# First mixer by feature halves: a column order of the modulation, written out by hand

## The chip, the cores and the metric

The kernel runs on one core of a Trainium2 chip. The metric is the device time of one execution in microseconds, median of the runs. The engines named below are TensorE (PE; its weight loads are PEld), VectorE (DVE), ScalarE (ACT), GpSimd (POOL) and SyncE (SP), which here issues nearly all loads.

## The reference, cut to what matters

Two transformer blocks run one after the other on 256 tokens of 1024 features. The first block takes a condition vector `c` and makes six rows of 1024 values from it (`mod = silu(c) @ w_ada + b_ada`, a matrix of 1024 x 6144). The change is about the first two, `shift_m` and `scale_m`:

```python
mod = (jax.nn.silu(c) @ w_ada[l] + b_ada[l])[:, None, :]
shift_m, scale_m, gate_m, shift_f, scale_f, gate_f = jnp.split(mod, N_MOD, axis=-1)
h = rms_norm(x, g_mix[l]) * (1.0 + scale_m) + shift_m
x = x + gate_m * hybrid_mixer(h, w_in[l], ...)
h = rms_norm(x, g_ffn[l]) * (1.0 + scale_f) + shift_f
x = x + gate_f * hierarchical_moe(h, ...)
```

The mixer multiplies `h` by `w_in` (1024 x 2896) and cuts the product into queries, keys and values of two attentions and into an indexer (`iq`, 512 columns; `ik` and its weights, 72 columns), which picks 64 keys for each token. The mixture of experts chooses 2 of 32 experts for each token; each expert has three matrices of 1 MB. The second block (a recurrent mixer and a dense feed-forward) is not touched by the change.

## The kernel before, in words

**Order.** The kernel is a straight-line program for the five engines. A planner, which has a cost for each instruction, puts the instructions into the queue of their engine. Instructions that are marked (`keep_in_program_order`; the helpers `held`, L76, and `held_pe`, L95, mark while the list `holding` is filled, with two entries also those of PE) stay in the order of the program text. All loads on SP are marked, so they are issued in the text's order, and each waits there until its buffer is free.

**Head of the first mixer.** `ada_piece` (L125) loads 1 MB of `w_ada`: 2 rows of each partition, 1024 columns of one of the six outputs, 4 KB a row. The head loads four pieces of output 0 (shift), then `xt` (the tokens, 1 MB, L158), four pieces of output 1 (scale), then the columns of `w_in` in 1 MB pieces with 2 KB rows. `ada(v)` (L328) multiplies each piece as it lands, four products of 32 rows side by side; after the fourth piece it copies the sums (L351) and turns them into columns with 16 products against `selh` (each 64 weight columns), and adds the bias (L357). Feature `f` lies on partition `f // 8`, so that a column of `w_in` needs all of `w_ada`'s columns of both outputs before any feature can be used. Meanwhile `xt` is normed (L395, L388, L437) and turned (L400). `scaled` (L414) makes the eight feature tiles: `hTh` on ACT (L423), `full` on DVE (L425), and the rest `hTl` on POOL or DVE (L426).

**Projections.** Every large product is made of three: high by high, high by low, low by high (`mm3`, L110). `hilo` (L85) cuts the weights: ACT copies the high part (L86), DVE subtracts (L87). One step of `proj_fm` (L467) is a cut of two feature tiles of 512 columns and 24 products of 256 columns; four steps make a projection. `proj_ik` (L498) does the 72 indexer columns and the 8 forget columns with 24 products. `main` runs one cut ahead of the products. The order of the work is a string of letters (L885): `iiqikqqFqXFXbb...`, i = indexer queries, q = queries of the second attention, k = `proj_ik`, F = a step of `forget` (its first turns the indexer's key and weights, L622 to L628, and then works on the forget gate), X = a step of the indexer for tokens 128 to 255 (the first makes the scores `p_dot`, L680, and ReLU, L681; then DVE sums them, L685, and picks the best 64 in 8 rounds, L691 and L692).

**Experts.** `load_experts` (L228) takes the 96 matrices in the order of 8 units of 4 experts, gates, then ups, then downs. The kind of buffer of load `i` is `RING[i % 21]`: 1 is a buffer of `raw`, 2 of `raw2`, 3 of `raw3`. 16 loads go out at the letter W, five more (L911) behind the first block's mixer, when `raw3` exists. `raw3` has five buffers, and the first of them holds `xn2`, the normed tokens, until they are cut into three parts (L1015 to L1019). The fifth of those loads, which is load 20, takes that buffer. Unit 0 then calls `load_experts` after its gates, its ups and its downs, four loads each (L1335 to L1351).

**Router.** Around L1041 everything is marked. The text has, for the second half of the tokens: squares, `turned`, `normed`, `warm(5)`, `logits(1)`, `experts(0)`, `rank(0)`, `warm(3)`, `places(0)`, `gather_t(0)`. `warm(n)` (L102) issues n constant products of 128 x 128.

## Time and profile before

| What | Value |
|---|---|
| median of 3 runs | 719.64 us (718.5 to 719.88) |
| the profiled execution's own time | 719.28 us |
| its span | 717.6 us |
| mean granted TensorE clock | 0.966 |
| PE busy | 651.5 us (91%) |
| DVE, ACT, POOL busy | 397.3, 301.2, 46.1 us |
| moved by DMA | 196.94 MB |

A row of the timeline gives start and duration in us, then engine, line and operation, what is written from what is read, its shape and how many; in square brackets stands the idle time of the engine ahead of it and what ended it. Fp32 products are recorded twice each, so 16 records are 8 products. Ends of PE instructions are modelled, starts are not. "x" behind a group counts records.

### The profile page before, as it was taken

What the parts mean: (1) busy time and instruction counts of PE and PEld (TensorE: products, weight loads), DVE (VectorE), ACT (ScalarE), POOL (GpSimd) and SP (SyncE); (2) the same over time, 40 slices, a digit from 0 to 9 for tenths busy, and PEclk for the clock granted to TensorE, in tenths of its full rate; (3) what the DMA queues carried; (4) which work ended last, traced back from release to release, by engine and by line L of the source; (5) the groups of instructions that cost most, each with busy time, mean ns of one, the idle gap of its engine ahead of it and who ended that gap; (6) DMA issues with size and microseconds to landing.
All of it is one profiled execution on the core that took longest, in us unless ns stands there. A gap on an engine that the chain in (4) does not pass through costs nothing. (4 is left out here: it accounts for less than half of the span.)

```text
span 717.6 us, 13286 instructions
## 1 busy us (share of the span) xinstructions
PE 651.5 (91%) x5485; PEld 508.2 (71%) x5485; DVE 397.3 (55%) x753; ACT 301.2 (42%) x505; POOL 46.1 (6%) x71
## 2 busy tenths in 40 slices
PE   4799999999988789569889999999999999999996
PEld 0498787767845454324545699987899999898994
DVE  2277967877651242123123489788575555555555
ACT  1456454654631020101101587756474444444445
POOL 7010000001000000000000423100000000000001
PEclk9899999999998999879999999999999999999998
DMA  9999669998579999999999997535346555550001
GB/s 340 374 375 393 229 261 333 306 419 295 226 317 416 418 419 418 414 418 398 418 418 393 377 365 295 177 117 167 128 141 206 194 196 200 168 187 1 1 1 58
DMA packets 69203, 196.94 MB, mean 274 GB/s; under 512 B 7550, under 2 KB 33219, under 8 KB 57350
## 3 DMA queue, kind: packets, MB, share of 16 engines
q1 hardware_dynamic: 67558, 195.30, 72.5%
q8 instruction: 53, 0.87, 0.5%
q10 hardware_dynamic: 1216, 0.30, 0.2%
q0 software_dynamic: 352, 0.28, 0.1%
q14 instruction: 24, 0.20, 0.1%
HBM read 194.81 MB, written 1.05 MB: 273 GB/s over the span
## 5 line engine op out<-in xcount | busy, mean ns | idle before, releaser
L100 PE MATMUL p_gu<-Xl,wguh 128*128 128x256 f32 x352 | 99.8, 284 | 0.0
L100 PE MATMUL p_gu<-Xh,wgul 128*128 128x256 f32 x352 | 99.3, 283 | 0.0
L100 PE MATMUL p_gu<-Xh,wguh 128*128 128x256 f32 x352 | 98.9, 283 | 0.1
L100 PEld LDWEIGHTS p_gu<-Xl,wguh 128*128 128x128 f32 x352 | 67.5, 192 | 0.5
L100 PEld LDWEIGHTS p_gu<-Xh,wguh 128*128 128x128 f32 x352 | 67.1, 192 | 0.7 <-ACT Xh L1392 0.4
L100 PEld LDWEIGHTS p_gu<-Xh,wgul 128*128 128x128 f32 x352 | 67.4, 192 | 0.3 <-DVE wgul L87 0.2
L100 PE MATMUL p_gu<-eg,xg 128*32 128x256 f32 x576 | 44.3, 467 | 22.1 <-PEq L1311 19.9
L100 PEld LDWEIGHTS p_gu<-eg,xg 128*32 128x32 f32 x576 | 24.0, 132 | 43.2 <-issue 36.1
L1163 ACT ACTIVATE sl<-p_gu 128x256 f32<-128x256 f32 x9 | 3.5, 384 | 121.5 <-PE p_gu L100 121.5
L1164 DVE TENSOR_TENSOR sl<-sl,p_gu 128x256 f32<-128x256 f32 x9 | 3.8, 421 | 79.5 <-ACT sl L1163 79.5
L87 DVE TENSOR_TENSOR wdnl<-wdn,wdnh 128x1024 fp32r<-128x1024 f32 x22 | 27.0, 1225 | 32.4 <-ACT wdnh L86 32.4
L100 PE MATMUL p_w<-hTh,wih 128*128 128x256 f32 x128 | 37.5, 296 | 2.5 <-ACT wih L86 2.5
L87 DVE TENSOR_TENSOR wgul<-wup,wguh 128x1024 fp32r<-128x1024 f32 x22 | 27.0, 1225 | 21.3 <-ACT wguh L86 20.2
L86 ACT ACTIVATE wdnh<-wdn 128x1024 fp32r<-128x1024 f32 x22 | 23.3, 1058 | 36.5 <-PE p_gu L100 35.9
L100 PE MATMUL p_dn<-ed,aT 128*32 128x512 f32 (+2 forms) x304 | 33.0, 573 | 5.9 <-ACT aT L1171 5.9
L87 DVE TENSOR_TENSOR wgul<-wgt,wguh 128x1024 fp32r<-128x1024 f32 x22 | 27.0, 1225 | 19.8 <-ACT wguh L86 19.8
L86 ACT ACTIVATE wguh<-wgt 128x1024 fp32r<-128x1024 f32 x22 | 23.3, 1061 | 33.7 <-PE p_gu L100 18.2
L100 PE MATMUL p_w<-Xh,w2h 128*128 128x256 f32 x128 | 37.0, 289 | 0.5 <-ACT w2h L86 0.3
L100 PE MATMUL p_w<-Xh,w2l 128*128 128x256 f32 x128 | 36.2, 284 | 0.6 <-DVE w2l L87 0.6
L100 PE MATMUL p_w<-hTl,wih 128*128 128x256 f32 x128 | 36.5, 287 | 0.0
L100 PE MATMUL p_w<-Xl,w2h 128*128 128x256 f32 x128 | 36.4, 284 | 0.1
L100 PE MATMUL p_w<-hTh,wil 128*128 128x256 f32 x128 | 36.2, 288 | 0.0
(624 smaller groups left out, 1546.4 us busy)
## 6 DMA issues: line engine op xcount, KB each, us to landing
eg<-in_w_gate_dram SPq DMA_DIRECT2D x32, 1024.0 KB
eu<-in_w_up_dram SPq DMA_DIRECT2D x32, 1024.0 KB
ed<-in_w_down_dram SPq DMA_DIRECT2D x28, 1024.0 KB
wada<-in_w_ada_dram SPq DMA_DIRECT2D x24, 1024.0 KB
w<-in_w_in_dram SPq DMA_DIRECT2D x11, 1024.0 KB
wgt<-in_w_gate_up_dram SPq DMA_DIRECT2D x11, 1024.0 KB
wup<-in_w_gate_up_dram SPq DMA_DIRECT2D x11, 1024.0 KB
wdn<-in_w_down_dram SPq DMA_DIRECT2D x11, 1024.0 KB
```

The costliest lines, as they stand in the source:

```text
L86: held(act.activation(hi, src, AF.Copy))
L87: held(eng.tensor_tensor(lo, src, f32(hi), op=OP.subtract))
L100: held_pe(pe.matmul(o, lhsT, rhs, start=start, stop=stop, skip_group_check=True))
L1163: act.activation(st.s[:st.n], st.b[:st.n, 0:256], AF.Silu)
L1164: dve.tensor_tensor(st.s[:st.n], st.s[:st.n], st.b[:st.n, 256:512], op=OP.mult)
```

## The change

It does these things:

- The feature order of the first mixer changes: feature `f` of half `h` lies on partition `(f - 512 h) // 4`, four to a partition in each half (`load_cols`, the biases, `turn_half`). Shift and scale come in halves of 512 columns (`ada_half`, two loads of 1 MB each, 2 KB rows; class `Cols` with its three steps `prod`, `cols`, `turn`; the turn has four products against `sel4`).
- The loads go in this order: scale half 0, `xt`, shift half 0, first half of `iq`'s rows, first half of `bq`'s rows, `wik`, `w_bf` (two loads), scale half 1, shift half 1, then the other halves of `iq` and `bq`.
- The head is written out in a fixed order on PE, ACT, DVE and POOL, up to the indexer's scores and ReLU; the indexer stands ahead of the rest of `bq`. The string starts with `qFFX` behind that.
- `RING` has 20 entries for the first pass, `AGAIN` has 21 for the later ones: load 20 takes a `raw` buffer (that of load 0), load 24 takes `xn2`'s. Unit 0 issues 4, then 5 loads.
- The router has `warm(1)` and `warm(2)` for `warm(5)` and `warm(3)`.

```diff
-RING = [1, 1, 2, 2, 1, 1, 1, 1, 1, 2, 1, 1, 2, 2, 1, 1, 3, 3, 3, 3, 3]
+RING = [1, 1, 2, 2, 1, 1, 1, 1, 1, 2, 1, 1, 2, 2, 1, 1, 3, 3, 3, 3]
+AGAIN = RING[:4] + [3] + RING[4:]
...
-    for _ in range(4):
-        ada_piece(0)
+    ada_half(1, 0)
     tc.keep_in_program_order(nc.sync.dma_start(xt, dram("x", 0, [[D, 128], [128 * D, 2], [1, D]])))
-    for _ in range(4):
-        ada_piece(1)
+    ada_half(0, 0)
+    w_iq = [load_cols("win768_0", 768, 512, 0)]
+    w_bq = [load_cols("win1352_0", 1352, 512, 0)]
+    w_ik = load_cols("wik", 1280, 72)
...
+    ada_half(1, 1)
+    ada_half(0, 1)
...
+    class Cols:
+        def __init__(self, v, h):
+            self.v, self.h, self.p = v, h, bank([128, 512], "p_ada")
+        def prod(self, q):
+            for r in range(4):
+                mm(self.p[32 * r:32 * r + 32], csr[:, 4 * q + r, :], wada[self.v, self.h][q][:, r], q == 0, q == 1)
+        def cols(self):
+            self.part = a1.tile([128, 512], FT, name="part", tag="fin", bufs=3)
+            held(act.activation(self.part.rearrange("p (j n) -> p j n", j=4),
+                                self.p.rearrange("p (n j) -> p j n", j=4), AF.Copy))
+        def turn(self):
...
+            for j in range(4):
+                mm(p[:, j:j + 1], self.part[:, 128 * j:128 * j + 128], sel4, j == 0, True)
+            held(dve.tensor_tensor(modcol[:, v, hs], p, bcol[:, v, hs], op=OP.add))
...
+    first[1].prod(0)
+    turn_half(0)
+    first[1].prod(1)
+    first[1].cols()
+    first[1].turn()
+    turn_half(1)
...
+    run = ahead_of(st)
+    tokens(range(2))
+    run()
+    tokens(range(2, 4))
+    for gen in (st, sq_):
+        ahead_of(gen)()
+    ik_ = cut_ik()
+    second = [Cols(1, 1), Cols(0, 1)]
+    second[0].prod(0)
+    second[0].prod(1)
+    second[0].cols()
+    run = ahead_of(sq_)
+    run(jjs=(0,))
+    second[0].turn()
+    second[1].prod(0)
+    second[1].prod(1)
+    second[1].cols()
+    run(jjs=(1,))
+    run = ahead_of(st)
+    second[1].turn()
+    prod_ik(*ik_, range(4))
+    tokens(range(4, 6))
+    run()
+    tokens(range(6, 8))
+    run, run2 = ahead_of(st), ahead_of(sq_)
+    run()
+    prod_ik(*ik_, range(4, 8))
+    run2()
+    next(gates)
+    next(index1)
...
-    for c in "iiqikqqFqXFXbbYYbb...":
+    for c in "qFFXbbYYbb...":
...
-    warm(5)
+    warm(1)
+    experts(0)
     logits(1)
-    experts(0)
     rank(0)
-    warm(3)
+    warm(2)
...
         gate_up(st, "u")
-        load_experts(n)
+        load_experts(n + (k == 0))
```

## Rows read from the trace of the kernel before

**Rows 1.** The page, its part with 40 equal slices of the span: PE and GB/s.

```profile
PE   4799999999988789569889999999999999999996
...
GB/s 340 374 375 393 229 261 333 306 419 295 226 317 416 418 419 418 414 418 398 418 418 393 377 365 295 177 117 167 128 141 206 194 196 200 168 187 1 1 1 58
```

**Rows 2.** Waits of SP's queue: us in total, times, longest.

```profile
SPq L252 <- DVE xn L1019: 20.4, 1, 20.4
```

**Rows 3.** Timeline of SP, loads of experts around the router.

```profile
177.78 1.97 SPq L252 DMA_DIRECT2D eu<-in_w_up_dram  x4
200.30 2.50 SPq L252 DMA_DIRECT2D ed<-in_w_down_dram  x4
```

**Rows 4.** Timeline of PE: first gates of the experts, downs of the last unit.

```profile
192.12 3.66 PE L100 MATMUL p_gu<-eg,xg 128*32 128x256 f32 x64
...
397.59 3.21 PE L100 MATMUL p_dn<-ed,aT 128*32 128x512 f32 x32 [0.53 <-ACT aT L1171]
```

**Rows 5.** Timeline of all engines, head of the first mixer.

```profile
17.18 1.06 ACT L395 ACTIVATE prob<-xt 128x1024 f32<-128x1024 f32 x1
...
22.06 0.75 DVE L437 TENSOR_SCALAR prob<-xt,rsr 128x1024 f32<-128x1024 f32 x1
...
28.25 1.06 PE L100 MATMUL p_ada<-wada,csr 128*32 128x512 f32 x8 [1.11 <-DMA wada<-in_w_ada_dram]
29.38 0.60 ACT L351 ACTIVATE part<-p_ada 128x512 f32<-128x512 f32 x1 [8.22 <-PE p_ada L100]
...
30.03 1.21 PE L100 MATMUL p_col<-selh,part 128*64 128x1 f32 x32 [0.72 <-ACT part L351]
...
33.68 1.23 DVE L87 TENSOR_TENSOR wil<-win,wih 128x1024 fp32r<-128x1024 f32 x1 [0.86 <-ACT wih L86]
...
33.70 0.58 PE L100 MATMUL p_w<-hTh,wih 128*128 128x256 f32 x1 [2.46 <-ACT wih L86]
...
34.90 1.07 ACT L86 ACTIVATE wih<-win 128x1024 fp32r<-128x1024 f32 x1
```

**Rows 6.** Windows of 5 us: busy us of PE, PEld, DVE, ACT, POOL, clock, DMA, GB/s.

```profile
10.00:15.00 5.00, 3.60 (x20) 0.40 (x16) 0.00 (x0) 0.00 (x0) 4.92 (x12) 1.00 1.03 410
...
40.00:45.00 5.00, 5.00 (x44) 5.00 (x44) 4.66 (x8) 2.99 (x4) 0.79 (x1) 1.00 1.04 376
...
70.00:75.00 5.00, 5.00 (x44) 5.00 (x43) 4.90 (x17) 2.04 (x3) 0.00 (x0) 1.00 0.62 216
```

**Rows 7.** Timeline of PE and ACT, from the indexer's keys to the next projection.

```profile
50.04 0.28 PE L100 MATMUL p_ik<-hTh,ikh 128*80 128x256 f32 x1
...
55.68 0.60 PE L100 MATMUL p_dup<-aqk,dup 80*128 80x256 f32 x2
...
59.70 2.00 PE L100 MATMUL p_dot<-aqk,iqT 64*128 64x256 f32 x16
...
62.25 2.04 ACT L681 ACTIVATE prob<-p_dot 128x512 f32<-128x512 f32 x4
...
62.69 0.38 PE L642 MATMUL p_lft<-ident,lf 128*8 128x128 f32 x2 [0.99 <-DVE lf L638]
...
62.83 0.36 PE L100 MATMUL p_w<-hTh,wih 128*128 128x256 f32 x1
```

**Rows 8.** Windows of 1 us, columns as in the windows of 5 us.

```profile
36.00:37.00 1.00, 1.00 (x6) 1.00 (x6) 1.00 (x2) 1.00 (x2) 0.74 (x1) 0.50 0.96 239
...
181.00:182.00 1.00, 1.00 (x7) 1.00 (x6) 0.86 (x6) 0.36 (x2) 0.00 (x0) 0.52 1.07 451
...
185.00:186.00 1.00, 1.00 (x11) 1.00 (x11) 0.00 (x0) 1.00 (x1) 0.00 (x0) 1.00 1.06 451
```

**Rows 9.** Timeline of PE and ACT in the router.

```profile
182.05 2.34 PE L108 MATMUL p_warm<-ones,ident 128*128 128x128 f32 x10
182.29 0.60 ACT L959 ACTIVATE h<-p_tr 128x512 f32<-128x512 f32 x1 [0.90 <-PE p_tr L561]
...
184.18 2.01 PE L100 MATMUL p_lg<-wr,h 128*128 128x36 f32 x16
```

## The prediction

> **What bounds the kernel now.** I read the page's slices first, then the waits of SP, then the timelines. In the slices [rows 1] the PE digit is 9 nearly throughout the second half of the span, where the loads are far from full: that part is PE's, and the change does not touch it. Slices 13 to 22 (the experts, about 200 to 390 us) are the ones with full loads, 414 to 419 GB/s, and a PE below 9. So the first question is which of the two sets the end of the experts.

> The loads have a hole: SP stands 20.4 us before one load for `xn2` [rows 2]. It is load 20, issued at 200.30, while the four before it went out at 177.78 [rows 3]. From 200.30 on, 76 MB are to come: 76 x 1.0486 MB at 418 GB/s [rows 1] are 190.7 us, which ends at 391, and some 2 us later the last piece has landed. PE wants the last downs at 397.59 and waits there for ACT's `aT`, not for a load [rows 4]. So the loads have about 4 us to spare, and the end of the experts is set by PE's own chain, which starts with unit 0's gates at 192.12 [rows 4]. What brings that start forward is gained; what brings only loads forward is not.

> The start at 192.12 hangs on the first mixer, where PE is busy in nearly every window from 40 us on, with DVE close by at 70 us (4.90 of 5) [rows 6]. Before that PE starves: its first projection product is at 33.70, 5.45 us behind the landing of the last of eight `w_ada` pieces at 28.25 [rows 5].

> **The head of the mixer.** *Loads.* Rows of 4 KB come at 410 GB/s (2.56 us a MB), the mix with 2 KB rows at 376 (2.79) [rows 6]. [...] I take 2.79. The fifth MB then lands near 17.8, against 28.25 for the ninth. `iq` and `bq` follow at 20.5 and 23.3. For `wik` and `w_bf`, small rows, I allow 2.5. The second halves of scale and shift land by 31.5 and 37.0, `iq`'s at 39.8, `bq`'s at 42.5.

> *Start.* `xt` is third and lands near 12.3. From the first square to the end of the second norm it was 17.18 to 22.81, 5.6 us [rows 5], so `xn` stands at 18.0. The text puts `turn_half(0)` ahead of the last shift product, so this product runs about 19 to 20.5, the copy takes 0.60, the turn less than the 1.21 of 32 small records [rows 5], since it has 8; the shift stands at 22.3. From there to steady products it was 2.4 us; I take 2.5. First products: 24.8, which is 8.9 ahead of 33.70.

> *From there to the indexer's scores.* Before, the scores `p_dot` came at 59.70 [rows 7]. Now PE has ahead of them: seven groups of 24 products; `proj_ik`, 24 more; four groups of `w_ada` products at 1.06 [rows 5]; two turns, 1.0 as an estimate from the 1.21; the duplication and turn of the keys, 0.7. From 50.04 to 55.68 [rows 7] there are 48 products, 0.1175 each, so a group takes 2.82, and the sum is 8 x 2.82 + 4.2 + 1.0 + 0.7 = 28.5. Before, six groups, `proj_ik` and the 0.7 were enough.

> *Waits that the fixed order adds.* ACT stands in text order. The copy `cols` of the second scale half comes ahead of the cut of `bq`'s next step, so that cut waits for the `w_ada` products, and PE for the cut: 0.60 + 1.07 + 1.23 [rows 5], about 2.9. Behind the ACT cut stand the next cuts and the tiles `hTh`. Before the second shift the cut's DVE half stands ahead of the bias addition: about 0.7. The duplicated keys need a copy, 0.4. Together 4.0: the scores at 57.3 with a full clock.

> *The clock.* [...] From 33.70 to 50.04 there are 120 products, 14.1 at 0.1175 each, so the fall cost 2.2. [...] Bounds: no fall, and two of 2.2; I take half a fall, 1.1. The scores: 58.4, 1.3 earlier.

> *Behind the scores.* Before, PE waited 0.99 for `lf` and took the next projection at 62.83, 3.1 behind the scores [rows 7]. Now the same group can follow right behind the 2.0 of the scores if its cut is done, at 60.4: 2.4 earlier. If the planner leaves the cut behind the four ReLUs (2.04) it is 0.5 + 2.04 + 1.07 + 1.23 = 4.8 behind: 0.4 later than before. I take the first, as nothing orders the cut behind the ReLUs. DVE's sums get their first ReLU about 3 us earlier than after 62.25 [rows 7], so DVE does not hold this back. From there the string and the work are the same and PE is full, so I carry 2.4 to the end of the mixer; bounds of this term, from two falls and a late cut to neither wait nor fall: 2.9 later, 5.5 earlier.

> **The router.** Ahead of `logits(1)` stood five constant products, 182.05 to 184.39; the tile they cover was done at 182.29 + 0.60 [rows 9]. With one product the logits can start at 182.9 in place of 184.18, 1.3 earlier, and the chain behind them follows. The three later ones stand beside DVE's ranks; one less is worth 0 to 0.3. I take 1.3. `experts(0)` is DVE work and only changes place in the text.

> **The ring.** Load 20 takes the buffer of a gate of unit 0, free when the gates end, 192.12 + 3.6 = 195.7; it went out at 200.30. The loads resume 4.6 earlier, beyond what the mixer gives. Load 24 now waits for `xn2`, but four loads (10 us) run before it. By the first part PE waits for none of these loads: 0, with 4.6 as the other end if it does. The additional biases and `sel4` lie ahead of the first piece's landing: ACT issues two more loads of about 0.5; the first products are then on time or 0.5 late, and not on the path, as `xt` is later.

> **Sum.** 2.4 + 1.3 = 3.7. The profiled execution has 719.28, 0.36 below the median of the three runs, so 715.6 for one like it, 715.9 for the median. A measurement of this kernel can tell about 0.2% from no change, 1.4 us.

> **Rivals.**
> 1. *The order fits*: the second halves arrive in time, PE neither waits nor loses its clock. Scores at 24.8 + 28.5 + 0.8 = 54.1, the mixer 5.5 earlier; with the router 6.8: 712.8. For it: 8.9 us of start. Against: the copy and cut in ACT's order.
> 2. *The experts are bound by loads after all*: then the ring's 4.6 counts too, 8.3 in all: 711.3. For it: full loads [rows 1]; against: no wait for them at 397.59 [rows 4].
> 3. *The constant products were needed*: the clock fell to 0.52 at 181 and was back at 1.00 by 185, behind them [rows 8]. If it stays low, the price is at least the 2.2 of the mixer's fall, and about 3 with the gathers and part of the gates: router 1.7 later, total 0.7 earlier, 718.9. [...]
> 4. *The fixed order is worse than the planner's* (slower): two falls of the clock and the cut of the next projection behind the ReLUs. Scores at 57.3 + 4.4 = 61.7, the next projection 4.8 later at 66.5, 3.7 behind 62.83; less 1.3 from the router: 722.0. It decides when that projection starts more than 2.7 us behind 62.83. For it: the new gap on ACT; against: 8.9 us of start.
> 5. *The head start is lost within the mixer*, to a late weight or to DVE at 70 us; the router's 1.3 stays: 718.3, no change that can be told.

> **Chances.** Forecast 0.50, rival 1 0.16, rival 2 0.06: faster 0.72. Rivals 3 and 5, 0.10 and 0.06: same 0.16. Rival 4: slower 0.12. The range 711.0 to 720.0 takes in all but rival 4 and the ends of the others. The forecast alone, from a whole fall more and from half the waits: 713.5 to 718.3.

> **What would show it.** Right: first `p_w` near 24.8, `p_dot` near 58, PE idle of 2 to 3 us behind the first `w_ada` products of the second half, unit 0's gates near 188.4, load 20 right behind those gates and still no wait for loads at the last downs. Wrong: `p_dot` behind 60 (rival 4), a clock of 0.5 at the gathers (rival 3), gates of later units that move by more than unit 0's (rival 2), or `p_dot` early and unit 0 not (rival 5).

## The result and the profile after

The changed kernel takes 728.14 us (median of 4 runs, 725.22 to 729.8) beside 719.07 for the kernel before in the same comparison: a ratio of 1.0118, interval 1.0097 to 1.0139. By the ratio it is slower by 8.5 us, above the range of the prediction. The profiled execution has 727.04 us, span 725.3, against 719.28 and 717.6.

The page's slices of the changed kernel [rows 1]: slices 13, 14, 20 and 21, in the experts, have a PE digit one lower than before, and slice 4 (about 54 to 73 us) has 7 for 9.

```profile
PE   4887999999997689579779999999999999999996
```

SP's wait for `xn2` is 1.9 us for 20.4 [rows 2], and load 20 goes out at 200.14, right behind unit 0's gates as foreseen, though no earlier than before, since the gates are late. First the waits of SP, then SP's timeline [rows 3]:

```profile
SPq L267 <- DVE xn L1115: 1.9, 1, 1.9
```
```profile
181.20 1.98 SPq L267 DMA_DIRECT2D eu<-in_w_up_dram  x4
200.14 2.46 SPq L267 DMA_DIRECT2D ed<-in_w_down_dram  x4
```

PE's timeline of the head and the scores [rows 5, 7]. The first steady projection product is at 24.82, the wait for the ACT cut stands where it was foreseen, the scores come at 59.25 for 59.70, and the next projection follows them at 61.18 for 62.83. Then PE stops 4.47 us for `lf` (0.99 before), and the second scores, at 68.69 before, are 5.3 us late. The changed kernel first, then the row of the kernel before:

```profile
24.82 0.38 PE L105 MATMUL p_w<-hTl,wih 128*128 128x256 f32 x1 [1.47 <-POOL hTl L463]
...
37.03 0.39 PE L105 MATMUL p_w<-hTh,wih 128*128 128x256 f32 x1 [1.71 <-ACT wih L91]
38.29 0.39 PE L105 MATMUL p_w<-hTh,wil 128*128 128x256 f32 x1 [0.76 <-DVE wil L92]
...
47.87 0.39 PE L105 MATMUL p_w<-hTl,wih 128*128 128x256 f32 x1 [1.46 <-POOL hTl L463]
...
59.25 2.00 PE L105 MATMUL p_dot<-aqk,iqT 64*128 64x256 f32 x16
61.18 0.39 PE L105 MATMUL p_w<-hTh,wih 128*128 128x256 f32 x1
...
63.52 0.38 PE L105 MATMUL p_bfr<-bfr,ones 1*128 1x8 f32 x2
68.37 0.59 PE L697 MATMUL p_lft<-ident,lf 128*8 128x128 f32 x2 [4.47 <-DVE lf L693]
...
74.01 1.33 PE L105 MATMUL p_dot<-aqk,iqT 64*128 64x128 f32 x16
```
```profile
68.69 1.16 PE L100 MATMUL p_dot<-aqk,iqT 64*128 64x128 f32 x16
```

ACT's timeline says why. The gate's Exp and Ln with their two table loads stand behind the scores' ReLU, the copies of `bqT` and a cut. In the kernel before the first table load goes out at 57.10, ahead of the scores, and the Ln at 62.12 is the last instruction ahead of the ReLU at 62.25 [rows 7]. The changed kernel first, then the kernel before:

```profile
62.91 0.60 ACT L544 ACTIVATE bqT<-p_w 128x512 f32<-128x512 f32 x1
63.51 1.06 ACT L91 ACTIVATE wih<-win 128x1024 fp32r<-128x1024 f32 x1
...
65.07 1.28 ACT L690 ACT_TABLE_LOAD   x1
...
66.59 1.28 ACT L691 ACT_TABLE_LOAD   x1
67.89 0.21 ACT L691 ACTIVATE na<-na 128x16 f32<-128x16 f32 x1
```
```profile
57.10 1.28 ACT L635 ACT_TABLE_LOAD   x1
...
62.12 0.22 ACT L636 ACTIVATE na<-na 128x16 f32<-128x16 f32 x1
```

After that wait the clock is granted at 0.50 until 74. In the router it falls between 183 and 184 and stays at 0.50 until past 193 (before, back at 1.00 by 185 [rows 8]). Windows of 1 us, columns as in [rows 6]:

```profile
68.00:69.00 1.00, 0.63 (x4) 0.55 (x5) 0.83 (x4) 0.10 (x1) 0.00 (x0) 0.50 1.06 422
...
73.00:74.00 1.00, 1.00 (x6) 0.78 (x4) 0.93 (x4) 0.10 (x1) 0.00 (x0) 0.50 0.58 234
...
183.00:184.00 1.00, 1.00 (x10) 1.00 (x9) 0.11 (x1) 1.00 (x4) 0.00 (x0) 0.81 0.95 393
...
190.00:191.00 1.00, 1.00 (x7) 1.00 (x6) 0.75 (x4) 0.36 (x1) 0.00 (x0) 0.50 1.03 434
```

PE's timeline of the router and the experts [rows 4, 9]: the first logits' product is at 182.22 for 178.81, 3.4 us late; the second 16 take 3.50 us for 2.01; unit 0's gates start 4.35 late; and the last downs 7.56 late, at 405.15. So three stretches lost: the mixer 3.4, the router 0.95, the experts 3.2.

```profile
182.22 2.38 PE L105 MATMUL p_lg<-wr,h 128*128 128x36 f32 x16 [1.09 <-DVE h L1057]
184.41 1.95 PE L615 MATMUL p_tr<-ident,xt 128*128 128x128 f32 x8
...
186.57 3.50 PE L105 MATMUL p_lg<-wr,h 128*128 128x36 f32 x16
...
196.47 3.66 PE L105 MATMUL p_gu<-eg,xg 128*32 128x256 f32 x64
...
250.70 1.70 PE L105 MATMUL p_gu<-eg,xg 128*32 128x256 f32 x25 [1.43 <-issue]
...
306.96 3.23 PE L105 MATMUL p_xg<-Pq,xn 128*128 128x128 bf16 x30 [1.77 <-issue]
...
372.34 4.50 PE L105 MATMUL p_gu<-eg,xg 128*32 128x256 f32 x40 [3.30 <-PEq L1407]
377.86 2.79 PE L105 MATMUL p_gu<-eg,xg 128*32 128x256 f32 x24 [1.03 <-issue]
...
395.90 3.66 PE L105 MATMUL p_gu<-eg,xg 128*32 128x256 f32 x64
...
405.15 3.21 PE L105 MATMUL p_dn<-ed,aT 128*32 128x512 f32 x32 [0.53 <-ACT aT L1267]
```

The experts' code is the same, yet PE stops inside runs of equal products, where it waits for nothing that the profile shows ("issue"). The kernel before has one such stop there:

```profile
320.82 3.89 PE L100 MATMUL p_gu<-eg,xg 128*32 128x256 f32 x36 [2.10 <-issue]
...
368.27 5.35 PE L100 MATMUL p_gu<-eg,xg 128*32 128x256 f32 x64 [3.25 <-PEq L1311]
...
388.34 3.66 PE L100 MATMUL p_gu<-eg,xg 128*32 128x256 f32 x64
```

The idle time is not all that is lost at such a place. From unit 6's gates to the last unit's it is 23.56 us in the changed kernel and 20.07 before, for a stop of 1.03: the clock, which falls at the jump in both, is at 0.50 from 371.5 to 381.5 in the changed kernel and from 369 to 372 before. (`after_pad`, further down, has no stop there and takes 21.22.) Windows of 5 us from about the same work on, the kernel before, then the changed one:

```profile
373.00:378.00 5.00, 5.00 (x94) 3.66 (x87) 0.41 (x1) 0.38 (x1) 0.00 (x0) 1.00 1.02 424
```
```profile
377.00:382.00 5.00, 4.14 (x44) 2.02 (x48) 0.00 (x0) 0.00 (x0) 0.00 (x0) 0.54 1.02 423
```

Below, "first logits" is the start of the router's first product, and "gates to gates" the time from unit 0's gates to the last unit's (196.2 us before, 199.4 after); both are those of the one profiled execution, while the median is of all n.

### The profile page after: what moved, and what is told of

It is laid out like the page before. It is cut to its first block, busy times and chain, and to the rows that moved or that the text cites. A ratio compares the mean times of both kernels' runs of the same rounds, so it can differ in the third digit from the quotient of the medians.

```text
span 725.3 us, 13209 instructions
## 1 busy us (share of the span) xinstructions
PE 655.2 (90%) x5443; PEld 511.2 (70%) x5443; DVE 400.1 (55%) x757; ACT 302.3 (42%) x507; POOL 46.5 (6%) x71
## 5 line engine op out<-in xcount | busy, mean ns | idle before, releaser
L105 PEld LDWEIGHTS p_gu<-Xl,wguh 128*128 128x128 f32 x352 | 67.5, 192 | 0.5
L105 PEld LDWEIGHTS p_gu<-eg,xg 128*32 128x32 f32 x576 | 22.4, 130 | 44.1 <-issue 36.6
L91 ACT ACTIVATE wdnh<-wdn 128x1024 fp32r<-128x1024 f32 x22 | 23.3, 1057 | 36.5 <-PE p_gu L105 35.9
L91 ACT ACTIVATE wguh<-wgt 128x1024 fp32r<-128x1024 f32 x22 | 23.3, 1061 | 33.7 <-PE p_gu L105 18.2
```

What stands on the lines that cost most here:

```text
L91: held(act.activation(hi, src, AF.Copy))
L105: held_pe(pe.matmul(o, lhsT, rhs, start=start, stop=stop, skip_group_check=True))
```

## The experiments

**1. The forget gate's second step three steps later, and the old router and ring in the changed kernel.**

```diff
-    for c in "qFFXbbYYbbv
+    for c in "qFXbbFYYbbv
...
-    warm(1)
-    experts(0)
+    warm(5)
     logits(1)
+    experts(0)
     rank(0)
-    warm(2)
+    warm(3)
```

`lft_late` has the first edit, `warm_old` the others, `late_warm` all of them; `ring_old` has the ring and the `load_experts(n)` of the kernel before.

> The changed kernel, with the turn of the forget gate (lft) two projection steps later in the string (qFXbbF for qFFXbb). Theory A (the new wait is the cause): PE's 4.47 us before lft shrink to under 1 us, the clock stays at 1.00 from 62 to 76 us, the mixer's end (first p_lg, 182.22 in the changed kernel) comes 5 to 7 us earlier, near 176, unit 0's gates near 190, and the time falls to 719 to 722 us. Theory B (the fixed order costs elsewhere, and the wait hides behind DVE): p_lg moves by less than 2 us and the time stays above 725 us.

> The changed kernel with the router of the kernel before (five and three constant products, ranks of the first half behind the logits). Theory A (the products held the clock up): the clock is back at 1.00 within 4 us of its fall, p_lg of the second half takes near 2.0 us and not 3.5, unit 0's gates start 13.3 us behind the first p_lg as before, not 14.25, so the time is about 1 us lower, 726 to 728 us. Theory B (the products only delay): the gates start 15 us or more behind the first p_lg and the time is 1 us higher, 728 to 730 us.

> The changed kernel with the ring of the kernel before (load 20 waits for xn2). Theory A (loads have slack, the ring is worth nothing): gates of all units and the time within 1 us of the changed kernel, 727 to 729 us. Theory B (the earlier loads help): 730 us or more, with PE waiting for the downs of the last unit. Theory C (the earlier loads crowd out the fetch of instructions in the experts): the units from the gates of unit 0 to those of unit 7 take 196 to 197 us in place of 199.4, and the time is 724 to 726 us.

> Both edits, lft two steps later and the router of the kernel before. Theory A (wait and router are separate terms): the gain of lft later and that of the old router add up, 717.5 to 721 us, unit 0's gates near 188 to 189.5. Theory B (the clock in the router follows from what the mixer's end leaves, not from the constant products): the same as lft later alone within 0.5 us.

| run | median, us (n) | ratio to before | first logits | gates to gates |
|---|---|---|---|---|
| lft_late | 731.54 (4) | 1.0176 [1.0143, 1.0209] | 182.28 | 202.9 |
| warm_old | 732.29 (4) | 1.0201 [1.0151, 1.0251] | 181.75 | 204.4 |
| ring_old | 728.01 (4) | 1.0122 [1.0066, 1.0178] | 181.24 | 203.2 |
| late_warm | 734.15 (4) | 1.0220 [1.0165, 1.0276] | 182.89 | 207.3 |

The ring is worth nothing that the times can tell: 1.0122 with the old one, 1.0118 with the new. (In the profile of `ring_old` the experts take 3.8 us more than in the changed kernel. Its stops are at the same products, idle for 5.23 us in all for 4.41, and the products behind the second one are slower too: unit 3's downs, at 309.56, take 5.77 us for 3.64.) `lft_late` does take the wait away (0.46 for 4.47, second scores at 70.20 for 74.01), and its output products start 6.5 us ahead of the changed kernel's and 3.1 ahead of those of the kernel before (143.02, 149.54, 146.16): with the wait gone, what the forecast carried along is there. Yet nothing is left at the logits, which move by 0.06 us, and by the ratios the run is slower than the changed kernel. Its timeline of PE and POOL shows two new waits: PE stands 1.50 us for the router's bias `rbb`, with the clock at 0.50 behind it (from 165 to 170, for 1.00 before), and the memset of `xn2`, on which the squares and all that follows hang, comes behind the very last output product (in the kernel before it comes at 175.52, and the last output product at 177.32), so the logits wait 3.35 for 1.09. `lft_late` first, then the kernel before:

```profile
143.02 0.48 PE L105 MATMUL p_wo<-woh,obT 128*128 128x512 f32 x1
...
163.47 0.61 PE L105 MATMUL p_rb<-ident,rbb 36*128 36x36 f32 x2 [1.50 <-DVE rbb L919]
...
178.53 0.40 PE L105 MATMUL p_wo<-woh,oaL 128*128 128x512 f32 x1
...
178.99 0.10 POOL L1006 MEMSET xn<- 128x1 f32 x1 [10.35 <-PE p_wo L105]
...
182.28 2.39 PE L105 MATMUL p_lg<-wr,h 128*128 128x36 f32 x16 [3.35 <-DVE h L1057]
```
```profile
146.16 0.48 PE L100 MATMUL p_wo<-woh,obT 128*128 128x512 f32 x1
...
175.52 0.10 POOL L910 MEMSET xn<- 128x1 f32 x1 [6.99 <-PE p_wo L100]
```

With the old products `warm_old` is back at 13.3 us from the logits to the gates, but it lost 5 us in the experts, and its time is above that of both theories; so is that of `late_warm`, whose experts take 207.3 us. The stops of `warm_old` are the hint. It has five constant products more than the changed kernel ahead of the experts, which the trace counts as ten records, and its three stops come nine or ten records earlier in the same runs of products (x34 for x25, x40 for x30, x33 for x24). `ring_old` and `lft_late`, with as many PE instructions as the changed kernel, have them within one record of the changed kernel's:

```profile
249.43 2.14 PE L105 MATMUL p_gu<-eg,xg 128*32 128x256 f32 x34 [1.86 <-issue]
...
306.77 4.42 PE L105 MATMUL p_xg<-Pq,xn 128*128 128x128 bf16 x40 [3.39 <-issue]
...
382.40 2.13 PE L105 MATMUL p_gu<-eg,xg 128*32 128x256 f32 x33 [1.96 <-issue]
```

So the stops stand at fixed places of PE's instruction stream. The DMA view of the changed kernel has a queue of its own for instructions (packets, MB, share of 16 engines):

```profile
q8 instruction: 54, 0.88, 0.5%
```

That is 16 KB a packet. In unit 2 of the changed kernel one packet moves in the window from 242.0 to 242.5, while PE stands at the jump over a body of code (until 245.43), and the next only in the one from 248.0; PE stopped after 38 records and went on at 250.70.

**2. The places alone.** Products in a branch body that is jumped over are not executed, but they move all code behind it.

```diff
 def branch(st):
     with tc.If(rv > SLOTS):
+        if st.u == 1:
+            warm(N)
         x = Unit()
```

N is 21 in `after_pad`, 43 in `before_pad`, 5 in `router_alone` and 16 in `mixer_alone`. 43 products are 172 instructions as the trace counts them, the 21 that the change takes out are 84, and together that is 256; that the places repeat after 256 was my assumption, which `before_pad` tests. The last two are the kernel before with the change's router, and the changed kernel with the old router and ring, both with the units' code kept at the old places.

> The changed kernel, with 21 constant products more in PE's stream, in the body of the first unit's branch, which is jumped over: nothing executed changes, but everything behind that body stands where it stands in the kernel before (the change had taken 21 such products out ahead of it: 5 of the router's, 16 small ones of the first mixer's turns). Theory A (the experts' 3.2 us are stalls at fixed places of PE's stream: with 5 products more, warm_old's three stalls came 9 or 10 records earlier, x34 for x25, x40 for x30, x33 for x24, and ring_old, with the same stream, had them at x25, x30, x24): the stalls of 1.43 (unit 2), 1.77 (behind the fallback) and 1.03 us (unit 6) are gone, one of 2 to 2.7 us stands in unit 4 with x36 behind it as in the kernel before; from the first unit's gates to the last one's 196 to 197.5 us for 199.4; 724.5 to 726 us. Theory B (the loads' order or the clock makes them): 199 us or more there, 728 us. The gates of unit 0 are at 196.5 by both.

> [...] Theory A: the stall of 2.10 us in unit 4 goes, and stalls like the changed kernel's come: about 1.4 in unit 2 with x25 behind, 1.8 behind the fallback with x30, 1.0 in unit 6 with x24; first to last gates 198.5 to 199.5 us for 196.2; 721.5 to 723 us. Theory B: the kernel before, 719.4 us, with its one stall at x36.

> The kernel before with the change's router alone (1 and 2 constant products for 5 and 3), and 5 products in the body jumped over so that the code behind stands where it stood. Theory A (the products held the clock): the clock stays at 0.50 from about 183 to past 190, the second part's 16 logits' products take about 3.5 us for 2.01, first logits' product to unit 0's gates 14.2 us for 13.31; experts 196.2 us; 720.0 to 721.0 us. Theory B (only the fewer products count): 12.1 us there, 718.2 us.

> The changed kernel with the old ring and the old router's products, and 16 products in the body jumped over so that the code behind stands as in the kernel before: what is left of the change is the first mixer. Theory A (three separate terms: mixer 3.4, router 0.95, experts' code places 3.2): the wait for lf of 4.5 us and the clock at 0.50 behind it, first logits' product at 181.5 to 182.5, 13.3 us from it to unit 0's gates, experts 196 to 197 us with the one stall in unit 4; 722.0 to 723.5 us. Theory B (the mixer moves the experts by another way than the code's places): experts 199 us or more, 726 us or more.

| run | median, us (n) | ratio to before | first logits | gates to gates |
|---|---|---|---|---|
| after_pad | 726.51 (6) | 1.0080 [1.0053, 1.0108] | 184.37 | 197.0 |
| before_pad | 722.53 (12) | 1.0039 [1.0021, 1.0056] | 179.32 | 201.6 |
| router_alone | 720.15 (12) | 1.0020 [0.9999, 1.0040] | 179.29 | 195.4 |
| mixer_alone | 725.58 (12) | 1.0067 [1.0041, 1.0093] | 181.06 | 195.0 |

Theory A of the places holds, to the very product. The kernel before, with nothing else changed, gets the changed kernel's three stops at the same products and loses 2.8 us (by the ratio, interval 1.5 to 4.0); the changed kernel gets the one of the kernel before. PE's timeline, `before_pad` first, then `after_pad`:

```profile
248.04 1.70 PE L100 MATMUL p_gu<-eg,xg 128*32 128x256 f32 x25 [1.33 <-issue]
...
304.45 3.36 PE L100 MATMUL p_xg<-Pq,xn 128*128 128x128 bf16 x30 [2.15 <-issue]
...
376.20 2.79 PE L100 MATMUL p_gu<-eg,xg 128*32 128x256 f32 x24 [0.93 <-issue]
```
```profile
326.30 3.48 PE L105 MATMUL p_gu<-eg,xg 128*32 128x256 f32 x36 [2.08 <-issue]
```

By the ratios, the three parts measured alone are 4.8 us (mixer), 2.8 (places) and 1.4 (router), together 9.0 beside the 8.5 of the whole; each has an interval of at least 1.2 us to either side, so the sum fits and proves little. By medians `after_pad` got back 1.6 us of the changed kernel's 728.14; its profile has the experts 2.4 us shorter and a head that lost as much, with the scores at 61.61 for 59.25. `before_pad`'s profiled execution is the slowest of its twelve (725.24), and its experts take 2 us more than theory A's upper bound; unit 6 alone takes 23.49 us to the last gates, as in the changed kernel, for 20.07. `router_alone` shows neither theory: 12.2 us from the logits to the gates as in theory B, yet no gain in the median. `mixer_alone` has the wait of 4.47 for `lf` and its experts as in theory A, but its median lies 2 us above A's range. The profiled executions of these two are the fastest of their twelve (717.82 and 718.99), so their profiles do not show what the medians lost.

**3. Places without stops, and the mixer's end.** If the stop depends on how soon behind the jump a packet ends, code can be laid so that none does.

```diff
     with tc.If(rv > SLOTS):
+        warm({4: 20, 5: 20, 6: 24}.get(st.u, 0))
...
-EoDEEESZpppp":
+EoDEEZESpppp":
...
+    load_experts(1)
     xn2 = raw3.tile([128, RAW], FT, name="xn2", tag="raw3").rearrange("p (t d) -> p t d", t=2)
     tc.keep_in_program_order(pool.memset(xn2[:, 0, 0:1], 0.0))
-    load_experts(RING.count(3))
+    load_experts(RING.count(3) - 1)
```

`before_places` is the kernel before with the first edit. `late_places` is `late_warm` with the old ring and the first edit (with 16 more in the body of unit 1), `late_rb` adds the second edit, `late_rb_xn` the third as well.

> The kernel before, with 20, 20 and 24 constant products in the bodies of the branches of units 4, 5 and 6, which are jumped over here: the same instructions are executed, and each of these units' code is laid so that a 16 KB piece of the instruction queue ends some 230 to 250 instructions behind the place where the jump lands, for 56 at unit 4. Theory A (a unit stalls where the piece in which its jump lands ends within about 5 us of work, since the next piece is asked for only some 6 us after the first: 312.5 and 318.0 us in the kernel before, 242.0 and 248.0 in the changed one): no stall of 1 us or more behind any jump, first to last gates 193.5 to 195 us for 196.2, 716.5 to 717.8 us. Theory B (the places had their effect by chance of the runs): 196 us, 719.3 us.

> The first mixer of lft_late (the forget gate's second step three steps later), with the old ring, the old router's products, and the units' code laid as in before_places. Theory A (the end of this mixer loses what the head gained: the wait for rbb with the clock at 0.50 behind it, and xn's memset that waits for the last product of the output): first logits' product at 182 to 183 us as in lft_late and late_warm, 13.3 us to unit 0's gates, experts 193.5 to 195.5 us with no stall; 719.5 to 722 us. Theory B (this mixer costs nothing by itself and late_warm's 14 us were all code places, 207 us there for 196): 716 to 718 us.

> late_places with the router's weights one step earlier, ahead of the last of attention a's steps. Theory A: no wait for rbb of over 0.3 us and the clock full from 160 to 175, so the output's products of part 1 start some 1.5 us earlier and run at 0.23 us each for 0.43 (13 of them, 2.6 us): first logits' product 3 to 4 us earlier, at 178.5 to 179.5; 716 to 718.5 us. Theory B (the clock falls at that place whatever waits, or the DVE work that was ahead of rbb makes another product late): within 1 us of late_places.

> late_rb with xn in the second slot of its ring and an expert's matrix in the first. Theory A (xn's memset waited for the last product because its slot lies on what that product reads): the memset is no longer behind the last output product, the wait ahead of the first logits' product is about 1.1 us for 3.35, the first logits' product at 176 to 177.5 us; 713.5 to 716.5 us, faster than the kernel before. Theory B (the second slot is freed no earlier, or the expert's load in the first slot waits and its unit starts late): not faster than late_rb, or slower by up to 2 us.

| run | median, us (n) | ratio to before | first logits | gates to gates |
|---|---|---|---|---|
| before_places | 716.52 (10) | 0.9951 [0.9933, 0.9969] | 179.26 | 193.7 |
| late_places | 721.47 (12) | 1.0041 [1.0011, 1.0071] | 186.79 | 192.4 |
| late_rb | 722.61 (12) | 1.0026 [1.0001, 1.0050] | 181.16 | 193.0 |
| late_rb_xn | 720.56 (12) | 1.0018 [0.9995, 1.0041] | 178.70 | 194.0 |

`before_places` executes what the kernel before executes and is 3.0 us faster by the medians. None of the four has an "issue" stop of PE in the experts. `late_places` lost 5.4 us of its profiled run in the head, where the clock had fallen (0.50 from 25 to 30 us and 0.62 from 40 to 45, for 1.00 in `late_warm`; scores at 65.35 for 59.92); its end has the two waits of `lft_late` again, 1.50 and 3.35. `late_rb` takes the first away, and the clock stays at 1.00 there (160 to 180); its time cannot be told from that of `late_places` and lies above theory A's. The second stayed in both, 3.37 and 3.51: the second slot of the ring is freed no earlier, theory B for that run.

**4. What was open: the router's term, and the mixer's.**

```diff
     spl = p1.enter_context(tc.tile_pool(name="spl1", bufs=3, side="right"))
+    for i in range(1):
+        for tag in ("hi", "lo"):
+            pool.memset(spl.tile([128, 1024], FR, name="turn", tag=tag)[:, 0:1].bitcast(FT), 0.0)
...
         held(dve.tensor_copy(iw, p[:, :, 64:80]))
-        yield
         p = bank([128, 8], "p_bfr")
...
-        act.activation(na, na, AF.Exp)
-        act.activation(na, na, AF.Ln, bias=1.0)
+        held(act.activation(na, na, AF.Exp))
+        held(act.activation(na, na, AF.Ln, bias=1.0))
```

`late_turn` is `late_rb` with the first edit; `early_places` adds the others (with the gate's DVE steps marked too, and "qFXbbYY" in the string). `router_places` is `before_places` with the change's router, 5 products going into the body of unit 1; `mixer_places` is `mixer_alone` with the bodies of `late_places`.

> before_places with the change's router (1 and 2 constant products for 5 and 3; the 5 missing ones stand in a body that is jumped over). Theory A (fewer products, and the clock where it was): first logits' product to unit 0's gates 12.1 to 12.3 us for 13.3, 715.3 us, a ratio about 0.0015 lower than before_places' 0.9951. Theory B (the products held the clock): the clock at 0.50 for 7 us or more between 183 and 194, 14 us there, 717 to 717.8 us. The spread of both should be within 2 us.

> mixer_alone with the units' code laid as in before_places. Theory A (the mixer's loss is the wait for lf and the clock behind it, in every execution): 2.5 to 3 us less than mixer_alone's 725.6, so 722.5 to 723.1, all executions within 3 us. Theory B (a good part is the head's clock, which falls in some executions only): the executions stand in two groups, one at 718 to 720 us, one 4 to 8 us above it.

> late_turn's kernel with the forget gate's first step undivided and in order: its Exp and Ln stand ahead of the scores' ReLU on ACT as in the kernel before, and PE goes on with the rest of the bq group. Theory A (the wait for lf is what the mixer loses in the middle): no wait of over 0.5 us for lf, second scores at 66 to 67.5 us for 68.69 in the kernel before and 74.01 in the changed one, first logits' product at 175 to 177; 713.5 to 716 us when the head's clock holds. Theory B (scores' ReLU 3 us later make DVE's ranking late, and what follows waits for it): a new wait of 2 us or more behind the scores, no faster than late_turn.

> late_rb with the pairs of split buffers turned by one (two one-element memsets at the start), so that xn's memset needs the first product of a weight's first quarter only, not the last output product. Theory A: memset ahead of the last output product, 1.1 us of wait ahead of the first logits' product for 3.37, that product 2.3 us earlier, at 176 to 177 us with a full clock in the head; 2 us less than late_rb_xn's 720.6, so 718 to 719. Theory B (the squares wait for DVE's sums instead): within 0.7 us of late_rb_xn.

| run | median, us (n) | lowest, highest | ratio to before | first logits |
|---|---|---|---|---|
| router_places | 716.31 (7) | 715.06, 718.35 | 0.9959 [0.9944, 0.9974] | 179.64 |
| mixer_places | 722.50 (12) | 716.54, 724.90 | 1.0037 [1.0015, 1.0059] | 184.67 |
| early_places | 719.89 (12) | 717.02, 727.10 | 1.0032 [1.0005, 1.0059] | 180.77 |
| late_turn | 714.75 (8) | 712.16, 718.50 | 0.9942 [0.9917, 0.9968] | 178.09 |

Turning the split buffers moved `xn2` off the last product's weights: in `late_turn` the logits wait for nothing, and the profiled run reaches unit 0's gates at 190.64, 1.5 us ahead of the kernel before, although its head lost clock (0.50 from 40 to 45 us, scores at 61.80). The median is over 3 us below the 718 to 719 of theory A. The profile shows one gain more than the wait of 3.37: from the logits to the gates it takes 12.6 us for 14.9 in `late_rb`, with the clock at 1.00 from 180 to 190 for 0.71 and 0.61. Why the clock held is not shown.

```profile
178.09 1.98 PE L105 MATMUL p_lg<-wr,h 128*128 128x36 f32 x16
...
190.64 3.66 PE L105 MATMUL p_gu<-eg,xg 128*32 128x256 f32 x64
```

So the change's head with three repairs (the gate's step later, the router's bias earlier, the buffers turned) and code places without stops beats both the kernel before and the changed one; beside `before_places` it is ahead in the median, but the intervals overlap. `early_places` failed: the gate's chain still stood behind the copies of `bqT` on ACT, PE waited 2.65 us for `lf`, and the ReLU began at 66.42. `mixer_places` is 6.0 us above `before_places`, with a spread of 8.4 us for 1.7 and no two clear groups: neither theory as it was put, though the median is A's. Its profile has both the wait for `lf` (4.46) and a head that lost clock (0.50 from 40 to 45; scores at 61.75), and its first logits come 5.4 us behind those of `before_places`. `router_places` is 0.2 us below `before_places` by the medians and 0.6 above by the ratios: the fewer products bring 12.2 us from logits to gates for 13.3 in the profile, and nothing in the time that can be told.

## Why the prediction was wrong

**The head of the mixer: right in the order of events, and in the number partly by luck.** Start 24.8 forecast, 24.82 found; the waits of the fixed order 2.9 forecast, 1.71 and 0.76 found; scores 58.4 forecast, 59.25 found, a miss of 0.85. The 2.2 for a fall of the clock is what the kernel before took from 33.70 to 50.04 beyond 0.1175 a product, with the clock at 0.50 from 31 to 37 us (one of these windows is in [rows 8]) and at 0.66 from 37 to 38; half of it was my choice between the bounds, and no run shows such a half. In this execution the clock did not fall (1.00 in every window of 1 us from 20 to 62), so the 1.1 for it was not spent; with a full clock the forecast was 57.3, a miss of 1.95. PE was busy for 30.50 us between its first product and the scores where the sum has 28.5, and idle for 3.92 where it has 4.0, though not at the same places: 1.46 of it is a wait for `hTl` that was not in the sum.

```profile
24.82:59.25 34.43, 30.50 (x249) 26.67 (x249) 16.07 (x25) 13.90 (x21) 3.75 (x8) 1.00 1.05 385
```

In other executions the clock did fall: 5 of 12 profiles of the changed head have the scores at 61.3 to 65.4 us for 58.8 to 59.9, while the five of the old head have them at 59.70 to 60.50. (`early_places` is not among the 12: it has 62.13 with a full clock.) Windows from 40 to 45 us, `after_pad`, then the changed kernel:

```profile
40.00:45.00 5.00, 5.00 (x23) 2.01 (x24) 0.32 (x2) 0.31 (x1) 0.00 (x0) 0.50 1.05 390
```
```profile
40.00:45.00 5.00, 5.00 (x44) 3.55 (x44) 1.24 (x3) 1.54 (x2) 0.00 (x0) 1.00 1.05 394
```

**Behind the scores: this step failed.** "From there the string and the work are the same and PE is full, so I carry 2.4 to the end of the mixer." In place of 2.4 early, the first logits' product came 3.4 late. The next projection did follow at once (61.18). But the text of the change splits `forget()` by a yield, which the diff of the change above does not print (it stands in experiment 4's): its bias product, its `z`, Exp and Ln no longer go out ahead of the scores, and the string, with "FF" behind the projection, asks for their result next. The 0.99 of wait that I saw in [rows 7] was the end of a chain that had been running beside the scores; the change took its cover away, and I took only the wait out. It became 4.47, then 6 us with the clock at 0.50 (68 to 74). `lft_late` shows that it is this wait: without it the output products start 3.1 us ahead of the kernel before. That its removal alone brought nothing is the end of the mixer (experiments 1, 3 and 4). The bounds of this step do not follow from its own terms either: by them the next projection starts between 6.7 us earlier (54.1 + 2.0) and 3.7 later (66.5, as in rival 4), for 5.5 and 2.9. And the 17.8 for the fifth MB of the loads comes out of no row (nine at 2.56 end at 28.25, so five at 2.79 end near 19.2); nothing hung on it, as the product for that piece, at 18.84, waited for no load.

**The router: size off.** 1.3 forecast; in the profile 0.95 lost, alone 1.4 lost with an interval that reaches no loss, on code without stops no difference that can be told. Rival 3 was half right: a clock of 0.61 or less over two stretches of 5 us in a row between 185 and 200 stands in 3 of 6 profiles with few products (the changed kernel, `lft_late`, `after_pad`) and in 1 of 12 with the old ones (`late_places`). In the changed kernel the clock is down to 0.81 in the window from 183 to 184, in the logits' products. `router_alone` and `router_places` have as few products and lost the clock for less (0.66 from 185 to 190 and 1.00 from 190 to 195 in both). What decides between the two courses stays open.

**The ring: right.** It let load 20 go right behind the gates, and it is worth nothing that can be told. The 2 us from the last bytes to the landing, in the sum for the loads' end, were my estimate. No run shows them for these loads; the nearest is the end of the kernel before, where the last bytes of the output move before 716.2 us and the span ends at 717.6.

**The experts: a term that I left out.** Nothing in them is edited, so I gave them 0. The change takes 21 products out of PE's stream ahead of them, which are 84 instructions (the trace counts two products for each, with a weight load apiece), and moves, by the estimate of a packet below, every jump's landing within its packet. That is 2.8 us, shown by `before_pad`, in place of 0. The one stop of 2.10 in the profile of the kernel before was the row that I passed over.

Rival 4 named the side but not the mechanism: its 722.0 came from two falls of the clock ahead of the scores and a late cut, and the cut was on time.

## What to carry to other kernels

A short wait on the critical engine can be the tail of a long chain that runs beside other work: before a step is moved ahead of it or split, ask when the chain's first instruction is now issued on each engine. When only the order or the number of instructions changes, look for "issue" stops inside runs of equal products, compare how many products stand behind them, and move the code by products in a body that is jumped over before judging the edit. A gain in the middle was kept here only once the tile that starts the next stage no longer lay on what the last product of this one reads, so look where that tile lies.
